# Power table of the S5 layer laid out power-innermost, and the SSD half of the output projection stored gated, with its input added

## Chip, cores and metric

One core of a Trainium2 chip runs the whole model in one launch. The metric is device time in microseconds; the kernel before was run three times (3845.32 to 3852.04, median 3851.29), and one further execution was profiled.

## What is computed

A two-layer model over 2048 latent tokens and 256 context tokens, 1024 features, float32. Layer one projects the normalised input, runs a bidirectional SSD (state-space) group and a windowed attention group with sinks beside it, and projects both together. Layer two is a bidirectional S5 layer (64 groups of 64 complex states, 16 channels) with GLU and gate. Cut to what the change touches:

```
def window_attention(q, k, v, kc, vc, sink):   # blocks of 128 queries
    kb, vb = band(k), band(v)                   # key block before, own, after
    ...                                         # plus all 256 context keys

def even_layer(x, xc, c, c_ctx, ...):
    shift, scale, gate = adaln(c, ada_w, ada_b)          # silu(c) @ ada_w + ada_b
    shift_c, scale_c, gate_c = adaln(c_ctx, ada_w, ada_b)
    ...
    x  = x  + gate   * (jnp.concatenate([ssd_out, att], -1) @ w_out)
    xc = xc + gate_c * (jnp.concatenate([ssd_c, att_c], -1) @ w_out)

def odd_layer(...):
    disc = s5_discretise(lam_re, lam_im, log_step, b_re, b_im)  # powers of ab below
    s_re, s_im, _ = s5_bidir(ug, disc, final_c)
    y = s5_output(s_re, s_im, ug, c_re, c_im, d_skip, glu_w, glu_b) * silu(g)
    x = x + gate * (y @ w_out)
```

## The kernel before

Tokens are handled in 18 tiles of 128 (`NT`; tiles 0 and 1 are context). Every float32 product is made of three TensorE products of a rounded and a residual part (`mm3`, lines 289 to 291); the parts are made by ScalarE (`Copy` to the rounded type) and by VectorE or GpSimd (`lo`, line 274).

The program is a chain of stages. In each, a main generator writes the stage's instructions and `merge` lets side generators put in theirs between, by a budget of modelled TensorE time (`self.pe`, the numbers after `yield`). TensorE's order is that of the writing; the other engines and the DMA queue (all loads and stores go through SyncE, SP below) are put in an order by a simulation of the program when it is built. Each engine works through its own list in order.

- **Attention**, about 1545 to 2350 us. For each query tile and head a score (`score`, lines 1154 to 1160: keys in rounded and residual form `K1`, `KL`, whose three band tiles sit in a ring of `RING` slots beside two context slots; a band that runs over the ring's end is read in two pieces), a softmax (1167, 1168), transposes (1174 to 1178) and the product with the values (1184). `kprep` writes the key tile two ahead. The side generator is `half_proj`: the SSD half of the output projection, 36 outputs of 128 x 512 (`f`, two halves of the columns by 18 tiles), copied from PSUM (line 1347) and stored to `part_d` in DRAM (1348). Between its outputs it computes 16 pieces of modulation (`ada_load`, `ada_mm`: 1024 KB of weights `aw` through one buffer, 32 small products, stored to `mod_d`): four pieces of layer one's gate, then twelve of layer two.
- **Output projection** (`out_proj`), about 2350 to 2690 us. Per tile it loads the input `xr` (1413) and the SSD half `pt` (1415), makes the attention half in PSUM (`ps`, eight times `mm3` for two halves), and for each half adds `pt` to it (VectorE, 1448), multiplies by the gate row (VectorE, 1449) and adds to `xr` (GpSimd, 1450; VectorE in the last tile). The sum is stored to `x1_d`, and ScalarE takes its square sum (1452).
- **S5 operators** (`s5_gen`), a side generator of the output projection and of the first part of layer two's input projection (`odd_proj`), about 2420 to 2905 us. VectorE makes powers 0 to 16 of the 64 x 64 complex eigenvalues by doubling (`pn`), copies them into `pw` (1553, 1555; the direction `d` = 1 backwards), and then for 16 pairs of groups and two directions makes the outer products `O` = C x power (1606 to 1611, 544 elements a partition) and `Gm` = B x power (1625 to 1627, 512 elements). In `pw` the 32 group pairs are innermost, so the power index has a step of 32 floats:

```
pw = cp.tile([P, 2, 2, 17, 32], F32, name="pw")
...
pv = lambda k: pw[:, k, d, ps0:ps0 + 16, p0:p0 + NB].rearrange("p t q -> p q t")[:, :, None, :].to_broadcast(sh)
...
V.tensor_tensor(g[:, k], bv(0), pv(x0), ALU.mult)
V.tensor_tensor(t, bv(1), pv(x1), ALU.mult)
```

`Gm` is transposed by TensorE (`gp`, 1639); `O` and B give the lag kernels (`gl`, 1658).

## Time and profile before

| | us |
|---|---|
| runs, lowest / median / highest | 3845.32 / 3851.29 / 3852.04 |
| the profiled execution, its own time | 3853.33 |
| its span in the profile | 3851.6 |
| TensorE busy over the span | 3454.3 (90%) |
| VectorE busy | 2555.0 (66%) |
| ScalarE busy | 1617.3 (42%) |
| GpSimd busy | 1167.9 (30%) |

The shares are means over stages that have different limits, so the stages are read apart, by windows of time. A busy TensorE is not TensorE at its peak: its products overlap, and their ends are modelled. Idle time of an engine that does not set the end costs nothing.

### The profile page before, as it was taken

Reading aid. Unit: us, or ns where it says so; the run is one execution under the profiler, and the core shown is the slowest. Engines: PE = TensorE matmul, PEld = TensorE weight load, DVE = VectorE, ACT = ScalarE, POOL = GpSimd, SP = SyncE. Lnnn points to the kernel's source line nnn. Section 1 sums busy time; section 2 is a strip of 40 time slices with the busy share of each in tenths; the row PEclk is TensorE's granted clock in tenths of the full one; section 3 lists DMA queues with packets and bytes.
Section 4 is the critical chain, followed back from the end, with each engine's and each line's share of the span. In section 5 each row is a group of like instructions: output and inputs, shape, how many; then the busy total and the mean of one; then the engine's idle time right before and its main releaser. Section 6 shows DMA issues by size and latency. Waiting matters only on the chain.

```text
span 3851.6 us, 68715 instructions
## 1 busy us (share of the span) xinstructions
PE 3454.3 (90%) x25669; PEld 3095.7 (80%) x25669; DVE 2555.0 (66%) x5430; ACT 1617.3 (42%) x3519; POOL 1167.9 (30%) x752
## 2 busy tenths in 40 slices
PE   6989899988999997989999999778799988989999
PEld 4978898978998886767877887556689978979977
DVE  5888876565435445756776777999895499503455
ACT  4544554543312223766667774222222522343321
POOL 3122234332213332375555532422101011132221
PEclk8989999999999998989999999889799999999999
DMA  7755577865666777564543336556878954895453
GB/s 282 229 201 187 191 231 261 258 227 193 225 229 217 264 244 210 151 176 129 147 114 102 98 91 183 166 167 197 240 243 264 301 189 143 270 291 165 127 164 110
DMA packets 664857, 758.28 MB, mean 197 GB/s; under 512 B 76795, under 2 KB 529339, under 8 KB 664523
## 3 DMA queue, kind: packets, MB, share of 16 engines
q1 hardware_dynamic: 664523, 753.88, 62.7%
q8 instruction: 203, 3.33, 0.4%
q14 instruction: 131, 1.07, 0.1%
HBM read 516.58 MB, written 237.15 MB: 196 GB/s over the span
## 4 chain that ended last, share of the span: by engine, by line
PE 34%; DVE 16%; DMA 8%; ACT 3%; issue 3%; SPq 3%; POOL 2%; DVEq 0%; POOLq 0%; ACTq 0%
PE mm L289 3%; PE mm L290 3%; PE mm L291 3%; PE pv L1184 3%; PE pt L1174 3%; PE S L1154 2%; PE gpo L289 1%; PE gpo L291 1%; PE gpo L290 1%; PE S L1156 1%; SPq L2023 1%; DVE sc L1884 1%; DVE Bu L1889 1%; DVE sc L1885 1%; DVE Gm L1625 1%
## 5 line engine op out<-in xcount | busy, mean ns | idle before, releaser
L289 PE MATMUL mm<-xTh,wh 128*128 128x256 f32 (+1 forms) x3320 | 1011.5, 305 | 73.5 <-ACT cR L603 24.7
L290 PE MATMUL mm<-xTl,wh 128*128 128x256 f32 (+1 forms) x3320 | 953.7, 287 | 1.3 <-POOL xTl L274 0.7
L291 PE MATMUL mm<-xTh,wl 128*128 128x256 f32 (+1 forms) x3320 | 953.1, 287 | 1.2 <-DVE wl L274 1.2
L289 PEld LDWEIGHTS mm<-xTh,wh 128*128 128x128 f32 (+1 forms) x3320 | 645.7, 194 | 105.2 <-ACT cR L603 27.0
L290 PEld LDWEIGHTS mm<-xTl,wh 128*128 128x128 f32 (+1 forms) x3320 | 645.5, 194 | 18.0 <-issue 14.7
L291 PEld LDWEIGHTS mm<-xTh,wl 128*128 128x128 f32 (+1 forms) x3320 | 643.8, 194 | 2.6 <-DVE wl L274 1.7
L1178 DVE TENSOR_TENSOR tl<-pt,th 128x512 fp32r<-128x512 f32 x328 | 223.7, 686 | 123.3 <-ACT th L1177 121.5
L1167 DVE TENSOR_SCALAR_CACHE_REDUCE p<-S,nsink 128x640 f32<-128x640 f32 (+2 forms) x288 | 235.1, 819 | 91.2 <-PE S L1156 89.1
L1168 ACT ACTIVATE p<-p,nm 128x640 f32<-128x640 f32 (+2 forms) x288 | 224.4, 779 | 91.5 <-DVE p L1167 89.8
L1174 PE MATMUL pt<-ident,p 128*128 128x128 f32 x1312 | 206.2, 280 | 38.9 <-DVE tl L1178 25.5
L1177 ACT ACTIVATE th<-pt 128x512 fp32r<-128x512 f32 x328 | 193.7, 593 | 110.9 <-PE pt L1174 107.5
L289 PE MATMUL mm<-wh,xTh 128*128 128x256 f32 x720 | 218.6, 304 | 16.4 <-DMA wh<-wk 8.6
L1174 PEld LDWEIGHTS pt<-ident,p 128*128 128x128 f32 x1312 | 158.0, 143 | 79.6 <-issue 35.1
L290 PE MATMUL mm<-wl,xTh 128*128 128x256 f32 x720 | 207.0, 287 | 1.6 <-POOL wl L274 1.0
L291 PE MATMUL mm<-wh,xTl 128*128 128x256 f32 x720 | 206.7, 287 | 0.0
L614 DVE SCALAR_TENSOR_TENSOR cA<-cR,vecs,cA 128x256 f32<-128x256 f32 (+3 forms) x192 | 184.6, 973 | 24.3 <-ACT cA L611 20.8
L946 DVE SCALAR_TENSOR_TENSOR rf<-rb,s_P,rf 128x128 f32<-128x128 f32 x288 | 123.8, 475 | 98.6 <-ACT rf L942 96.3
L401 POOL TENSOR_TENSOR xin<-xin,shr 128x1024 f32<-128x1024 f32 x33 | 88.1, 2680 | 316.1 <-DVE xin L400 311.2
L289 PEld LDWEIGHTS mm<-wh,xTh 128*128 128x128 f32 x720 | 141.5, 197 | 23.7 <-DVE zt L577 9.5
L274 POOL TENSOR_TENSOR wl<-w,wh 128x1024 fp32r<-128x1024 f32 (+1 forms) x43 | 99.9, 2326 | 193.9 <-ACT wh L282 163.4
L576 ACT ACTIVATE tz<-mm 128x256 f32<-128x256 f32 x144 | 54.2, 378 | 227.5 <-PE mm L291 227.4
L1184 PE MATMUL pv<-th,vv 128*128 128x512 f32 x328 | 147.8, 451 | 1.7 <-ACT sA L1116 1.0
(459 smaller groups left out, 9057.2 us busy)
## 6 DMA issues: line engine op xcount, KB each, us to landing
wh<-wk SPq DMA_DIRECT2D x116, 512.0 KB
wl<-wk SPq DMA_DIRECT2D x116, 512.0 KB
wk<-wh SPq DMA_DIRECT2D x56, 512.0 KB
wk<-wl SPq DMA_DIRECT2D x56, 512.0 KB
w<-in_e_w_in_dram SPq DMA_DIRECT2D x40, 512.0 KB
xin<-in_x_dram SPq DMA_DIRECT2D x38, 512.0 KB
rf<-prow_d SPq DMA_DIRECT2D x72, 256.0 KB
rb<-prow_d SPq DMA_DIRECT2D x72, 256.0 KB
```

The source lines that it names most:

```text
L274: eng.tensor_tensor(out, x, hi.bitcast(F32), ALU.subtract)
L289: mm(ps, lhsT=ah, rhs=bh, start=first, stop=False)
L290: mm(ps, lhsT=ah, rhs=bl, start=False, stop=False)
L291: mm(ps, lhsT=al, rhs=bh, start=False, stop=last)
L614: nc.vector.scalar_tensor_tensor(acc[:, q:q + m], R[:, s + j:s + j + m], cw[:, 12 * j + b:12 * j + b + 1], acc[:, q:q + m], op0=ALU.mult, ...
L946: V.scalar_tensor_tensor(rf[:, h], rb[:, h], self.s_P[:, c, 16 + hh:17 + hh], rf[:, h], op0=ALU.add, op1=ALU.min)
L1167: V.tensor_scalar(p[:, :w], s, -0.125, nsink[:, h:h + 1], op0=ALU.mult, op1=ALU.min, accum_out=nm)
L1168: A.activation(p[:, :w], p[:, :w], AF.Exp, bias=nm, scale=-1.0, accum_out=d["sm"][:, h:h + 1])
L1174: T.transpose(pt[:, n, :], Ps[h4][:, j * P:(j + 1) * P], self.ident)
L1177: A.activation(th, pt, AF.Copy)
L1178: V.tensor_tensor(tl, pt, th.bitcast(F32), ALU.subtract)
L1184: T.matmul(pv, lhsT=VV[kt][:, hk, :], rhs=t.rearrange("p a b -> p (a b)"), start=first and x == 0, stop=last and x == 1)
```

## The change

- `s5_gen`: `pw` becomes [.., 32, 17], the power innermost; four copies with permuted or reversed addresses take the place of the one at 1553 and the seventeen at 1555; the readers `pv` follow.
- `half_proj`: the output is multiplied by the gate row on its way out of PSUM and the input `xr3` is added by GpSimd before the store. So the four gate pieces come first, each behind a wait of modelled time; a gate row `g3` and an input tile `xr3` (one buffer each) are loaded.
- `out_proj`: `xr` is no longer loaded; VectorE multiplies PSUM by the gate and adds `pt`, two instructions as before; GpSimd's addition is gone.
- `RING` is 5.

```diff
@@ -1037,7 +1037,7 @@
 
         nc, i, tc = self.nc, self.i, self.tc
         V, G, A, T = nc.vector, nc.gpsimd, nc.scalar, nc.tensor
-        RING = 6
+        RING = 5
         with ExitStack() as st:
             e = st.enter_context
 
@@ -1330,12 +1330,24 @@
                     X = xprep(0)
                     z = None
                     if half == 0:
-                        yield ("until", self.pe + HL)
+
+                        for _ in range(4):
+                            z = ada_load()
+                            yield ("until", self.pe + HL)
+                            ada_mm(z)
+                            yield 1.5
+                        z = None
+                    gate = hp.tile([P, 512], F32, name="g3", bufs=1)
+                    self.modrow(gate, "e", 1, 2, half * 512, 512)
                     for t in range(NT):
                         if z:
                             ada_mm(z)
                             yield 1.5
                         z = ada_load() if t + 1 < NT else None
+                        xr = hp.tile([P, 512], F32, name="xr3", bufs=1)
+                        nc.sync.dma_start(xr, (i["ctx"][t * P:(t + 1) * P] if t < 2 else i["x"][(t - 2) * P:(t - 1) * P])[:, half * 512:half * 512 + 512])
+                        if t == 2:
+                            self.modrow(gate, "e", 0, 2, half * 512, 512)
                         xh, xl = X
                         if t + 1 < NT:
                             X = xprep(t + 1)
@@ -1344,7 +1356,8 @@
                             self.mm3(ps, xh[:, k, :], xl[:, k, :], W[k][0], W[k][1], k == 0, k == 7)
                             yield 0.65
                         y = hp.tile([P, 512], F32, name="y3", bufs=2)
-                        V.tensor_copy(y, ps)
+                        V.tensor_tensor(y, ps, gate, ALU.mult)
+                        G.tensor_tensor(y, y, xr, ALU.add)
                         nc.sync.dma_start(self.part_d[t * P:(t + 1) * P, half * 512:half * 512 + 512], y)
                         yield 0.2
             ORDER = [q for q in range(2, NT) if q < CTX] + [0, 1] + [q for q in range(2, NT) if q >= CTX]
@@ -1410,7 +1423,6 @@
         for t in range(NT):
             xh, xl = X
             xr = row("xr")
-            nc.sync.dma_start(xr, i["ctx"][t * P:(t + 1) * P, :] if t < 2 else i["x"][(t - 2) * P:(t - 1) * P, :])
             pt = row("pt")
             nc.sync.dma_start(pt, self.part_d[t * P:(t + 1) * P, :])
             if t + 1 < NT:
@@ -1445,9 +1457,8 @@
                     yield 0.43
             for h in range(2):
                 hs = slice(h * 512, h * 512 + 512)
-                V.tensor_tensor(pt[:, hs], ps[h], pt[:, hs], ALU.add)
-                V.tensor_tensor(pt[:, hs], pt[:, hs], gate[:, hs], ALU.mult)
-                (V if t == NT - 1 else G).tensor_tensor(xr[:, hs], xr[:, hs], pt[:, hs], ALU.add)
+                V.tensor_tensor(xr[:, hs], ps[h], gate[:, hs], ALU.mult)
+                V.tensor_tensor(xr[:, hs], xr[:, hs], pt[:, hs], ALU.add)
             nc.sync.dma_start(self.x1_d[t * P:(t + 1) * P, :], xr)
             A.activation(pt, xr, AF.Square, accum_out=ss[:, t:t + 1])
             if t == 1:
@@ -1549,10 +1560,11 @@
             V.tensor_tensor(o(1), o(1), t1[:, :m], ALU.add)
             m *= 2
 
-        pw = cp.tile([P, 2, 2, 17, 32], F32, name="pw")
-        V.tensor_copy(pw[:, :, 0], pn[:, :, :, 0:32])
-        for t in range(17):
-            V.tensor_copy(pw[:, :, 1, 16 - t, :], pn[:, :, t, 32:64])
+        pw = cp.tile([P, 2, 2, 32, 17], F32, name="pw")
+        for k in range(2):
+            V.tensor_copy(pw[:, k, 0].rearrange("p q t -> p t q"), pn[:, k, :, 0:32])
+            w = pw[:, k, 1]
+            V.tensor_copy(bass.AP(tensor=w.tensor, offset=w.offset + 16, ap=[list(w.ap[0]), [-1, 17], [17, 32]]), pn[:, k, :, 32:64])
         V.tensor_copy(self.AR, pn[:, 0, 16, :].rearrange("p (a b) -> p a b", a=2))
         V.tensor_scalar(self.AI[:, 0], pn[:, 1, 16, :].rearrange("p (a b) -> p a b", a=2), -1.0, None, op0=ALU.mult)
         V.tensor_copy(self.AI[:, 1], pn[:, 1, 16, :].rearrange("p (a b) -> p a b", a=2))
@@ -1600,7 +1612,7 @@
                 Os.append(O.rearrange("p k q t c -> p k q (t c)"))
                 sh = [P, NB, 17, 16]
                 t = wk.tile(sh, F32, tag="Ot", name="Ot", bufs=1)
-                pv = lambda k: pw[:, k, d, :, p0:p0 + NB].rearrange("p t q -> p q t")[:, :, :, None].to_broadcast(sh)
+                pv = lambda k: pw[:, k, d, p0:p0 + NB, :, None].to_broadcast(sh)
                 cv = lambda k: C[:, k, p0:p0 + NB, None, :].to_broadcast(sh)
                 for (k, x0, x1, s) in ((0, 0, 1, None), (1, 1, 0, -1.0)):
                     V.tensor_tensor(O[:, k], cv(0), pv(x0), ALU.mult)
@@ -1619,7 +1631,7 @@
                 sh = [P, NB, 16, 16]
                 t = wk.tile([P, NB, 17, 16], F32, tag="Ot", name="Ot", bufs=1)[:, :, 0:16, :]
                 ps0 = 0 if d == 0 else 1
-                pv = lambda k: pw[:, k, d, ps0:ps0 + 16, p0:p0 + NB].rearrange("p t q -> p q t")[:, :, None, :].to_broadcast(sh)
+                pv = lambda k: pw[:, k, d, p0:p0 + NB, None, ps0:ps0 + 16].to_broadcast(sh)
                 bv = lambda k: Bb[:, k, d, p0:p0 + NB, :, None].to_broadcast(sh)
                 for (k, x0, x1, op) in ((0, 0, 1, ALU.subtract), (1, 1, 0, ALU.add)):
                     V.tensor_tensor(g[:, k], bv(0), pv(x0), ALU.mult)
```

TensorE at the place where `half_proj` begins, before (`f` is an output of the SSD half, `wh`, `wl` the weights, `x3h`, `x3l` the transposed SSD output, `S` a score, `pt` the transposed softmax, `pv` the product with the values):

```order
9314 L1160 LDWEIGHTS identb
9315 L1160 MATMUL S<-maskb,identb 128x128
9316 L1154 MATMUL S<-K_17000,sA 128x256
9317 L1156 MATMUL S<-KL,sA 128x256
9318 L1174 MATMUL pt<-ident,p 128x128 x4
9319 L289 MATMUL f<-wh_17146,x3h 128x512
9320 L290 MATMUL f<-wl_17147,x3h 128x512
9321 L291 MATMUL f<-wh_17146,x3l 128x512
```

And with the change (`af` is a piece of the modulation, `aw` its weights, `cvs` the conditioning vector):

```order
9314 L1160 LDWEIGHTS identb
9315 L1160 MATMUL S<-maskb,identb 128x128
9316 L1154 MATMUL S<-K_17000,sA 128x256
9317 L1156 MATMUL S<-KL,sA 128x256
9318 L1174 MATMUL pt<-ident,p 128x128 x4
9319 L365 MATMUL af<-aw,cvs 32x64 x32
9320 L1184 MATMUL pv<-th,vv 128x512
9321 L1184 MATMUL pv<-tl,vv 128x512
```

Where the first output of the SSD half began now stands the first of four gate pieces; 46 to 57 other rows lie between one and the next, and the first `f` comes after the fourth. From the first product of the output projection on, TensorE's order is the same as before.

GpSimd at the end of the attention and the start of the output projection, before (`gt`, `o`: the attention's own gate and output; `x3p`: the transposed attention output, residual part):

```order
438 L1225 TENSOR_TENSOR o<-o,gt 128x1024
439 L274 TENSOR_TENSOR x3p<-x_27072,x3p 128x1024
440 L274 TENSOR_TENSOR x3p<-x_27150,x3p 128x1024
441 L1450 TENSOR_TENSOR xr<-xr,pt 128x512 x2
442 L274 TENSOR_TENSOR x3p<-x_27290,x3p 128x1024
443 L1450 TENSOR_TENSOR xr<-xr,pt 128x512 x2
444 L274 TENSOR_TENSOR x3p<-x_27358,x3p 128x1024
445 L1450 TENSOR_TENSOR xr<-xr,pt 128x512 x2
```

And with the change (`y`: the tile on its way to `part_d`):

```order
471 L1224 TENSOR_TENSOR gt<-gt,rb__26809 128x1024
472 L1225 TENSOR_TENSOR o<-o,gt 128x1024
473 L1360 TENSOR_TENSOR y_26932<-y_26932,xr_26708 128x512
474 L1360 TENSOR_TENSOR y_27130<-y_27130,xr_26947 128x512
475 L274 TENSOR_TENSOR x3p<-x_27249,x3p 128x1024
476 L274 TENSOR_TENSOR x3p<-x_27324,x3p 128x1024
477 L274 TENSOR_TENSOR x3p<-x_27461,x3p 128x1024
478 L274 TENSOR_TENSOR x3p<-x_27526,x3p 128x1024
```

The pairs `xr` between two `x3p` are gone, and the additions to `y` stand in the attention's list instead, 36 of them, between the rotations of queries and keys and the gates.

The DMA queue SP in the attention, with the change (line numbers of the changed kernel; before, 1348 was the store to `part_d`):

```order
1025 L1296 DMA an<-in_o_norm_w_dram 128x1x64
1026 L1361 DMA part_d<-y_19009 128x512
1027 L1348 DMA xr_19137<-in_x_dram 128x512
1028 L1324 DMA x_19450<-ysT_d 128x8x128
1029 L1292 DMA ab<-in_o_ada_b_dram 128x1x64
1030 L1075 DMA sin<-in_k_sin_dram 128x128
```

A store to `part_d` now waits for GpSimd's addition where it waited for VectorE's copy, and the load of the next `xr` stands right behind it.

## Rows read from the trace of the kernel before

**Rows 1.** busy us by stage: window, length, PE, PEld, DVE, ACT, POOL, clock, DMA, GB/s

```profile
1545.00:2350.00 805.00, 751.22 (x5522) 617.74 (x5521) 570.52 (x1178) 558.27 (x1124) 402.59 (x237) 0.98 0.45 121
2350.00:2425.00 75.00, 65.56 (x276) 51.15 (x275) 52.76 (x107) 26.47 (x34) 23.21 (x13) 0.91 0.90 268
2425.00:2690.00 265.00, 196.81 (x1169) 151.25 (x1168) 255.10 (x316) 51.68 (x104) 88.24 (x39) 0.87 0.54 168
2690.00:2925.00 235.00, 197.92 (x1899) 183.38 (x1898) 213.02 (x282) 63.34 (x153) 10.53 (x4) 0.89 0.82 248
```

**Rows 2.** the chain that ended last, shares by line, 2350 to 2930 us

```profile
by line: DVE Gm L1625 8.1%; issue 7.8%; DVE Ot L1626 6.8%; DVE O L1606 4.8%; DVE Gm L1627 4.5%; DVE Ot L1607 4.5%; PE mm L289 3.4%; DVE pt L1449 3.2%; PE mm L290 3.2%; PE mm L291 3.1%; DVE pt L1448 2.9%; DVE O L1609 2.8%; DMA xin<-x_d 2.3%;
```

**Rows 3.** TensorE by line, 2425 to 2690 us (count, busy us, mean ns, idle before)

```profile
L1639 PE MATMUL gp<-ident,Gm 128*128 128x128 f32 x108 | 22.0, 321 | 60.2 <-DVE Gm L1627 60.2
```

**Rows 4.** VectorE by line and form, 2425 to 2690 us

```profile
L1625 DVE TENSOR_TENSOR Gm<-Bb,pw 128x512 f32<-128x512 f32 x33 | 41.9, 1314 | 3.6 <-PE gp L1639 3.6
L1626 DVE TENSOR_TENSOR Ot<-Bb,pw 128x512 f32<-128x512 f32 x30 | 33.9, 1132 | 0.6
L1606 DVE TENSOR_TENSOR O<-C,pw 128x544 f32<-128x544 f32 x32 | 31.0, 1009 | 0.0
L1449 DVE TENSOR_TENSOR pt<-pt,gate 128x512 f32<-128x512 f32 x28 | 26.4, 956 | 0.0
L1607 DVE TENSOR_TENSOR Ot<-C,pw 128x544 f32<-128x544 f32 x31 | 25.2, 814 | 0.6
L1627 DVE TENSOR_TENSOR Gm<-Gm,Ot 128x512 f32<-128x512 f32 x30 | 23.8, 794 | 0.7
L1448 DVE TENSOR_TENSOR pt<-ps,pt 128x512 f32<-128x512 f32 x27 | 18.1, 682 | 2.2 <-PE ps L291 2.2
```

**Rows 5.** the same, 2690 to 2925 us

```profile
L1626 DVE TENSOR_TENSOR Ot<-Bb,pw 128x512 f32<-128x512 f32 x34 | 36.7, 1079 | 0.7
...
L1607 DVE TENSOR_TENSOR Ot<-C,pw 128x544 f32<-128x544 f32 x33 | 23.8, 723 | 0.7
L1627 DVE TENSOR_TENSOR Gm<-Gm,Ot 128x512 f32<-128x512 f32 x34 | 23.4, 688 | 0.6
L1606 DVE TENSOR_TENSOR O<-C,pw 128x544 f32<-128x544 f32 x32 | 21.6, 717 | 0.3 <-PE gl L1658 0.3
```

**Rows 6.** GpSimd additions among VectorE's work (start us, us)

```profile
2488.31 3.29 POOL L1450 TENSOR_TENSOR xr<-xr,pt 128x512 f32<-128x512 f32 x2 [1.32 <-DVE pt L1449]
2488.70 1.78 DVE L1609 TENSOR_TENSOR O<-O,Ot 128x544 f32<-128x544 f32 x1
...
2490.52 1.67 DVE L1607 TENSOR_TENSOR Ot<-C,pw 128x544 f32<-128x544 f32 x1
```

**Rows 7.** GpSimd by line and form, 2425 to 2690 us

```profile
L1450 POOL TENSOR_TENSOR xr<-xr,pt 128x512 f32<-128x512 f32 x26 | 46.5, 1799 | 48.0 <-DVE pt L1449 35.5 <-DMA lag_d<-lg 12.5
L274 POOL TENSOR_TENSOR x3p<-x,x3p 128x1024 fp32r<-128x1024 f32 x12 | 41.0, 3414 | 121.0 <-ACT x3p L1392 81.4 <-DVE pt L1448 13.6 <-issue 13.2
```

**Rows 8.** single lines over the run (ns: least, median, greatest; first and last start)

```profile
L1449 DVE TENSOR_TENSOR pt<-pt,gate x36: 674/680/2915, 2382.0 to 2684.1; 128x512 f32<-128x512 f32 x36
...
L1450 POOL TENSOR_TENSOR xr<-xr,pt x34: 1282/1680/2891, 2382.7 to 2672.1; 128x512 f32<-128x512 f32 x34
...
L1555 DVE COPY pw<-pn x17: 181/184/2385, 2358.4 to 2460.6; 128x64 f32<-128x64 f32 x17
```

**Rows 9.** VectorE by line and form, 1545 to 2350 us

```profile
L1347 DVE COPY y<-f 128x512 f32<-128x512 f32 x36 | 24.7, 687 | 5.8 <-PE f L291 5.4
```

**Rows 10.** TensorE: a score in three pieces, then one in two (start us, us)

```profile
2199.92 0.22 PE L1154 MATMUL S<-K,sA 128*128 128x128 f32 x1
...
2200.81 0.60 PE L1174 MATMUL pt<-ident,p 128*128 128x128 f32 x4
...
2250.64 0.34 PE L1154 MATMUL S<-K,sA 128*128 128x384 f32 x1
...
2251.40 0.39 PE L289 MATMUL f<-wh,x3h 128*128 128x512 f32 x1
```

## The prediction

> **What bounds the kernel now.** I read busy time by stage first [rows 1], since the shares of the whole span mix stages with different limits. In the attention (1545 to 2350 us) TensorE is busy 751 of 805 us, VectorE 571, GpSimd 403: TensorE sets the pace and the other two have room. From 2425 to 2690 us, call it stage A, it is the other way round: VectorE is busy 255 of 265 us, TensorE 197, at a granted clock of 0.87, and GpSimd 88. From 2690 to 2925 us, stage B, VectorE has 213 of 235 us, TensorE 198, and the DMA engines a share of 0.82, so three resources lie close together. Next the chain of waits from 2350 to 2930 us [rows 2]: its three heaviest lines that belong to the S5 generator are the `Gm` products 1625 and 1626 (14.9% together) and the `O` product 1606; 1449 of the output projection has 3.2%. TensorE's waits say the same from its side: in A it stood 60.2 us before the transposes of `Gm`, and VectorE's 1627 released it [rows 3]. So in A a microsecond of VectorE is about a microsecond of the program, in B less, and in the attention nothing.
>
> **The power layout.** In `Gm` the innermost operand index is the power, and its step was 32 floats. Where GpSimd is nearly idle 1626 takes 1079 ns for 512 elements; 1627, the same number of elements with no such step, takes 688 ns [rows 5]. The product 1606 works on the same table, but there the power is not the innermost index, and 544 elements take 717 ns [rows 5]. So I charge the difference of 0.39 us to the step, and expect 1625 and 1626 at 0.69 us after. They run 63 times in A [rows 4]: 63 x 0.39 = 24.6 us. The loops make 64 of each, 128 in all, so some 65 are left for B: 25.4 us. The `O` products change only in a middle step: nothing. The building of `pw` had seventeen copies of a median 184 ns [rows 8], 3.1 us, and one larger; the four new copies have permuted addresses, which no row shows. Four of 544 elements cost at most 4 x 1.08 = 4.3 us by 1626, at least nothing: I take no change, and 4 us lie inside the range.
>
> **The gated half.** In the output projection VectorE had two instructions an output half (1448 and 1449) and has two after, both of 512 elements: no change, except that in the last tile the two additions of line 1450 that ran on VectorE go, 2 x 0.7 = 1.4 us by the length of 1448 [rows 4]. What goes besides is GpSimd's addition. GpSimd is not the bound, but its additions lengthen VectorE's instructions: next to one pair of 1450, which took 3.29 us, a 1609 took 1.78 us and a 1607 1.67 us [rows 6], where 1607 alone takes 0.72 [rows 5]. That is about 1.0 us for each addition, and with 26 in A [rows 7] 26 us. The other way: the mean of each form in A [rows 4] over its mean in B [rows 5], or over its median [rows 8] for 1449, and 1079 for 1625, times its count, gives 7.8 (1625) + 1.6 (1626) + 9.3 (1606) + 7.7 (1449) + 2.8 (1607) + 3.2 (1627) = 32.4 us, and of GpSimd's time in A 1450 had 46.5 of 87.5 us [rows 7], the residual parts `x3p` the rest, which stay: 0.53 x 32.4 = 17 us. I take 20 us, nearer to the count over all instructions than to the one pair.
>
> A page makes this term larger. The Trainium skill ("SBUF — State Buffer", section "SBUF: two separate sides") says that GpSimd and a VectorE instruction with two SBUF inputs take a shared port pair as an exclusive lock for a whole instruction. By it each addition could hold VectorE up for its full length; what that would give is the third rival, from rows alone. At the one pair shown the trace comes near it, 1.0 us for an addition that takes at least 1.28 [rows 8]; over all instructions it does not.
>
> Stage A therefore loses 24.6 + 20 + 1.4 = **46 us** of VectorE work. VectorE then needs 209 of the 219 us that are left (its 10 us of idle time kept), and TensorE's 197 us, which the low clock of 0.87 has stretched, still fit: VectorE stays the bound, so I count all of it. In stage B TensorE has at most 37 us of room and the DMA engines 0.18 x 235 = 42 us, and both are needed by the projection whose order does not change; of the 25.4 us I count half, **13 us**, with 0 and 25 as ends. In the burst at the start of the output projection, with a DMA share of 0.90 [rows 1], the loads of the first `xr` go, 512 KB each at 268 GB/s or 2 us; some additions go too. TensorE is busy 66 of 75 us there, so I take **1 us**, between 0 and 5.
>
> **What the attention pays.** Multiplying on the way out of PSUM costs VectorE what the copy did (687 ns [rows 9] against 682 for 1448, also PSUM with one SBUF operand [rows 4]). The 36 additions are at least 1.28 us each [rows 8], 46 us more for a GpSimd busy 403 of 805: hidden, if none holds others up. The input comes in 36 loads of 256 KB instead of 18 of 512, the same bytes, at a DMA share of 0.45 [rows 1]; SP issues 18 more and four gate rows. With a ring of five, five of the inner query tiles have a band over the end instead of four, and the last tile's band is cut too: 2 tiles x 16 heads. A score in three pieces takes 0.89 us from its first product to what follows, one in two 0.76 [rows 10]: 32 x 0.13 = 4 us of the engine that sets the pace. The four gate pieces come first, behind one weight buffer: 1024 KB at 121 to 268 GB/s [rows 1] is 4 to 9 us, and the next load can start only when the last piece is done. Some 50 other rows of TensorE lie between two pieces, which should cover most; three waits of 0 to 9 us are 0 to 27, and I take 4, near the lower end because that other work is there. In all **8 us** lost.
>
> **Sum.** 3853.3 (the profiled execution) - 46 - 13 - 1 + 8 = 3801; the median of the runs shown is 2 us under that execution, so 3799, and I say 3800. Its own range reaches from 3765 (26 instead of 20, all of B, 5 at the start, nothing paid: 3851 - 52 - 25 - 5 = 3769, less the 4 us of copies) to 3826 (17 instead of 20, nothing in B, 15 paid, 4 for the copies: 3851 - 43 - 1 + 15 + 4).
>
> **Rivals.**
> - *TensorE and the DMA engines take over early.* TensorE's order keeps `Gm` transposes among the projection's products, and each must still wait for the last of its VectorE chain; speaking for it: 197 busy of 265 us in A, and B's three near-limits. Against: the 60 us before 1639. Two thirds of A, nothing of B: 3851 - 30 - 1 + 8 = 3828.
> - *The layout saves nothing*, because the other operand of `Gm`, B with a broadcast inner index, makes it slow. For it: no row shows that broadcast alone in `Gm`. Against: 1606 has such a broadcast, at 717 ns. Left are 20 + 1.4 + 1 less 8: 3837.
> - *Each addition of 1450 had held VectorE for its whole length.* 26 x 1.28 = 33 us [rows 7, 8] instead of 20: 3787. For it, besides the page: greatest durations of 2.9 us in 1449 beside a median of 0.68 [rows 8]. Against: the 32.4 us counted above for all GpSimd work together.
> - *Slower: the chain behind an output.* PSUM, multiply, GpSimd add, store: the store to `part_d` stands in SP before loads of queries and keys, and waits for a GpSimd whose list holds rotations of 128 x 1024 elements. If an output is late by x, what the next query tile loads is late too, and TensorE, the bound there, stands. 36 outputs x 2 us = 72: 3872. It decides from 51 / 36 = 1.4 us an output. Against it: queries are loaded a tile ahead, and GpSimd is idle half of the time.
>
> **Chances.** The forecast 0.53; TensorE and DMA early 0.20; the lock 0.13; the layout 0.07; slower 0.07. The range 3765 to 3832 (the first rival with 4 us for the copies) takes in the forecast and the two at 0.20 and 0.13, 0.86 together, and leaves the other two out. A measurement of this kernel tells about 0.2%, some 8 us, from no change. Faster by more holds in all cases but the slower one, 0.93, less their edges: 0.92. That one is split: a mild form ends within 0.2%, 0.03 with the edges, and slower keeps 0.05.
>
> **What would show it.** Right: 1625 and 1626 at a median near 0.69 us, GpSimd in A below 50 us, means of 1606 and of the multiply near their medians, A shorter by 40 to 50 us at a higher clock, the wait before the `Gm` transposes well under 60 us, the attention longer by under 15. Wrong: 1625 still at 1.08; A shorter by less than 30 with TensorE busy throughout; waits of TensorE in the attention behind `af` or behind scores whose keys or queries came late; SP waiting for GpSimd before stores to `part_d`.

## Result and profile after

The changed kernel takes 3786.77 us (median of 4 runs, 3782.45 to 3792.56) against 3851.66 for the kernel before beside it: ratio 0.9831, 95% interval 0.9817 to 0.9845, 65 us faster. The profiled execution took 3789.91 us, its span 3788.1 (before 3851.6); TensorE is busy 3447.3 us of it (91%), VectorE 2477.5 (65%), ScalarE 1614.5 (43%), GpSimd 1146.1 (30%).

To see where 63.5 us of span went I cut both traces at marks that do not depend on time: the first score and the last product with the values bound the attention, the first and last product of the output projection bound the next stage, and the piece of layer two's input projection that still runs beside the S5 generator lasts until layer two's first `ips` product (called the odd stage below; it contains stage B). Windows of the kernel before (window, length, busy time of PE, PEld, DVE, ACT, POOL, then granted clock, DMA share, GB/s; in the rows PE is TensorE and PEld its weight loads, DVE is VectorE, ACT ScalarE, POOL GpSimd):

```profile
1525.70:2349.70 824.00, 760.35 (x5570) 625.88 (x5568) 585.70 (x1200) 572.13 (x1152) 417.66 (x252) 0.97 0.46 125
2356.10:2674.10 318.00, 251.34 (x1375) 192.63 (x1376) 288.02 (x398) 70.19 (x124) 110.33 (x51) 0.88 0.60 184
2674.10:2977.60 303.50, 256.29 (x2406) 239.16 (x2405) 248.69 (x321) 81.93 (x192) 23.25 (x10) 0.90 0.82 250
```

The same three of the changed kernel:

```profile
1534.30:2337.10 802.80, 755.59 (x5634) 629.68 (x5633) 583.18 (x1200) 568.30 (x1152) 462.57 (x288) 0.98 0.52 141
2344.70:2619.90 275.20, 245.34 (x1376) 190.34 (x1377) 237.82 (x385) 73.26 (x127) 45.94 (x18) 0.93 0.60 181
2619.90:2920.60 300.70, 258.86 (x2406) 239.81 (x2405) 216.45 (x314) 80.06 (x189) 21.01 (x8) 0.90 0.82 250
```

Attention 21.2 us shorter, output projection 42.8, odd stage 2.8. What is left (8.6 us more ahead of the attention, 6.5 less behind the odd stage, 1.2 more between two stages) lies in unchanged code. It looks like scatter between executions: no edit of this document lies ahead of the attention, and yet in the twelve profiles its first score starts anywhere from 1520.6 to 1536.5 us. Two things deserve a look. In the output projection VectorE lost 50 us of work and the stage 43 us. In the attention TensorE's busy time hardly moved (760 to 756, although it has 64 more products), so most of the 21 us is idle time that went: 63.7 us of it before, 47.2 after. I had forecast a loss there.

VectorE by line and form in the changed kernel, 2400 to 2635 us, which answers to [rows 4] (1637 to 1639 are the former 1625 to 1627, 1618 and 1619 the former 1606 and 1607, 1460 and 1461 the former 1448 and 1449):

```profile
L1637 DVE TENSOR_TENSOR Gm<-Bb,pw 128x512 f32<-128x512 f32 x36 | 29.6, 866 | 1.8 <-PE gp L1651 1.8
...
L1461 DVE TENSOR_TENSOR xr<-xr,pt 128x512 f32<-128x512 f32 x30 | 23.7, 808 | 0.0
L1618 DVE TENSOR_TENSOR O<-C,pw 128x544 f32<-128x544 f32 x32 | 23.4, 765 | 0.3 <-PE gl L1670 0.3
L1638 DVE TENSOR_TENSOR Ot<-Bb,pw 128x512 f32<-128x512 f32 x31 | 23.4, 753 | 0.6
...
L1460 DVE TENSOR_TENSOR xr<-ps,gate 128x512 f32<-128x512 f32 x30 | 20.2, 684 | 9.3 <-PE ps L291 9.2
```

The means are still above 0.69 us because of a few long instructions; least, median and greatest over the whole run show it. From the views of single lines, first the kernel before:

```profile
L1625 DVE TENSOR_TENSOR Gm<-Bb,pw x64: 1017/1084/3298, 2468.7 to 2896.2; 128x512 f32<-128x512 f32 x64
L1626 DVE TENSOR_TENSOR Ot<-Bb,pw x64: 1006/1086/2209, 2493.0 to 2917.3; 128x512 f32<-128x512 f32 x64
L1553 DVE COPY pw<-pn x1: 714/714/714, 2456.9 to 2456.9; 128x1088 f32<-128x1088 f32 x1
```

and the changed kernel:

```profile
L1637 DVE TENSOR_TENSOR Gm<-Bb,pw x64: 677/684/2910, 2452.5 to 2828.1; 128x512 f32<-128x512 f32 x64
L1638 DVE TENSOR_TENSOR Ot<-Bb,pw x64: 675/691/2718, 2471.4 to 2849.8; 128x512 f32<-128x512 f32 x64
L1460 DVE TENSOR_TENSOR xr<-ps,gate x36: 673/682/693, 2367.1 to 2623.6; 128x512 f32<-128x512 f32 x36
L1461 DVE TENSOR_TENSOR xr<-xr,pt x36: 673/680/2893, 2368.6 to 2625.4; 128x512 f32<-128x512 f32 x36
L1565 DVE COPY pw<-pn x2: 666/668/671, 2437.2 to 2444.2; 128x544 f32<-128x544 f32 x2
L1567 DVE COPY pw<-pn x2: 691/692/692, 2437.7 to 2444.7; 128x544 f32<-128x544 f32 x2
```

TensorE's wait before the transposes of `Gm`, 60.2 us before [rows 3], is 24.0 in the window 2400 to 2635 us:

```profile
L1651 PE MATMUL gp<-ident,Gm 128*128 128x128 f32 x112 | 20.9, 302 | 25.8 <-DVE Gm L1639 24.0 <-ACT Gev L1655 1.6
```

In that window GpSimd has, apart from one small memset, only the residual parts of [rows 7] left, at 2.7 us each instead of 3.4:

```profile
L274 POOL TENSOR_TENSOR x3p<-x,x3p 128x1024 fp32r<-128x1024 f32 x13 | 35.4, 2726 | 165.0 <-ACT x3p L1405 165.0
```

GpSimd's 36 additions now stand in the attention and cost there what was expected of them (window 1534 to 2337 us):

```profile
L1360 POOL TENSOR_TENSOR y<-y,xr 128x512 f32<-128x512 f32 x36 | 46.5, 1291 | 61.0 <-DVE y L1359 33.4 <-PE pt L1174 15.4 <-PE S L1156 11.6
```

### The profile page after: what moved, and what is told of

Same layout as the page of the kernel before. It is cut to its first block, busy times and chain, and to the rows that moved or that the text cites. A ratio compares the mean times of both kernels' runs of the same rounds, so it can differ in the third digit from the quotient of the medians.

```text
span 3788.1 us, 68824 instructions
## 1 busy us (share of the span) xinstructions
PE 3447.3 (91%) x25733; PEld 3100.0 (82%) x25733; DVE 2477.5 (65%) x5414; ACT 1614.5 (43%) x3519; POOL 1146.1 (30%) x754
## 3 DMA queue, kind: packets, MB, share of 16 engines
q1 hardware_dynamic: 667691, 754.93, 63.5%
q14 instruction: 131, 1.07, 0.1%
## 4 chain that ended last, share of the span: by engine, by line
PE 30%; DVE 13%; DMA 7%; SPq 2%; issue 2%; ACT 2%; POOL 1%; DVEq 0%; ACTq 0%; POOLq 0%
PE pv L1184 3%; PE pt L1174 3%; PE S L1154 2%; PE mm L289 2%; PE gpo L291 2%; PE gpo L290 2%; PE gpo L289 2%; PE S L1156 2%; PE mm L290 2%; PE mm L291 2%; DVE sc L1896 1%; PE f L289 1%; PE f L291 1%; PE f L290 1%; DVE sc L1899 1%
## 5 line engine op out<-in xcount | busy, mean ns | idle before, releaser
L946 DVE SCALAR_TENSOR_TENSOR rf<-rb,s_P,rf 128x128 f32<-128x128 f32 x288 | 135.0, 514 | 97.8 <-ACT rf L942 92.1
L408 PE MATMUL tp<-ident,xin 128*128 128x128 f32 x432 | 93.9, 304 | 63.7 <-DVE xTl L274 44.8
```

The lines of the kernel that those rows point to most:

```text
L946: V.scalar_tensor_tensor(rf[:, h], rb[:, h], self.s_P[:, c, 16 + hh:17 + hh], rf[:, h], op0=ALU.add, op1=ALU.min)
```

## Experiments

### The change in its parts

Four kernels from the kernel before: the power layout alone; the gated half with the gate pieces that it needs and the ring of five, in the old layout; the ring alone; the gate pieces alone, drawn ahead of the half product. Each edit is the piece of the diff above that its name says; the last two are short:

```diff
 r_only, of the kernel before
-        RING = 6
+        RING = 5
...
 q_only, of the kernel before
                     if half == 0:
-                        yield ("until", self.pe + HL)
+                        for _ in range(4):
+                            z = ada_load()
+                            yield ("until", self.pe + HL)
+                            ada_mm(z)
+                            yield 1.5
+                        z = None
```

> The kernel before with the power layout alone; everything else as before. If the parts simply add, this run has 63 x 0.39 = 25 us of the output projection's gain and about 3 us of the stretch behind it: 28 us less than before, the attention the same to 5 us, the median of the Gm products 0.69 us, GpSimd's additions still lengthening the multiply of the output projection (mean above 0.9 us). Rival: GpSimd's additions hide what the layout saves (a shorter list on VectorE runs into them more often): less than 15 us. Second rival: VectorE was the only bound and the additions cost nothing: 45 us or more.

> The kernel with the change, but with the power layout as before: the gated half with its input and the ring of five. If the parts add: 65 - 28 = 37 us less than before, of which some 20 in the attention and 18 to 22 in the output projection. If the attention's 21 us in the one trace are chance, 15 to 20 us in all.

> The kernel before with a ring of five key tiles, nothing else. By the count of extra score pieces 32 x 0.13 = 4 us slower. Rival: the other order that the build gives to the engines' lists makes the attention shorter, which would be up to 20 us faster; in that case the gain of the attention is the list's and not the gated half's.

> The kernel before with the four gate pieces written ahead of the SSD half, nothing else (the half is still copied and stored ungated, the ring is six). Theory: the attention's gain comes from this order, because the modulation pieces no longer stand between the outputs in the first half and the outputs spread more evenly: 10 to 20 us faster than before, all of it before the output projection. Rival: the pieces wait for their weights, as the prediction had it: 0 to 8 us slower. Second rival: no difference, and the gain comes from the gating or the ring.

Measured beside 19 runs of the kernel before (median 3849.79 us; the last row beside 4, as above); stage lengths from one profiled execution of each, which need not be a typical one: that of the layout alone is the slowest of its six runs (3836.18 us, median 3826.15), that of the gated half the fastest of its six (3816.35, median 3823.97).

| kernel | ratio, 95% interval | attention | output projection | odd stage |
|---|---|---|---|---|
| before | 1 | 824.0 | 318.0 | 303.5 |
| power layout alone | 0.9938 (0.9915 to 0.9962) | 821.7 | 302.2 | 293.3 |
| gated half, ring of five | 0.9931 (0.9911 to 0.9950) | 802.3 | 297.4 | 311.4 |
| ring of five alone | 0.9953 (0.9935 to 0.9970) | 804.8 | 318.7 | 305.6 |
| gate pieces first alone | 1.0013 (0.9999 to 1.0027) | 816.0 | 318.7 | 306.1 |
| all | 0.9831 (0.9817 to 0.9845) | 802.8 | 275.2 | 300.7 |

The layout and the gated half each shorten the output projection, by 15.8 and 20.6 us, and the two together by 42.8. The layout alone gave less there than the 25 us expected: with GpSimd's additions still in place the multiply 1449 rose from 32.4 to 37.7 us of VectorE, so part of what the `Gm` products saved seems to have gone to instructions that now met the additions; without the additions the layout is worth 22.2 us (297.4 to 275.2). By the medians the two parts give 24 and 26 us (28 and 37 were expected), 49 together, and the whole change 65. 6.4 us of that difference lie in the output projection, as just read; where the rest lies is not shown. The gate pieces give nothing that can be told from no change, so the expected 10 to 20 us did not come. The surprise is the ring: a number that I had costed only by its extra score pieces makes the kernel 19 us faster by itself, and the attention 19 us shorter; in the two other kernels that have it the attention is 21 to 22 us shorter.

### Why a shorter ring helps

A ring of five gives TensorE more to do, so the gain must be a wait. ScalarE works its list in the order of the build. In the attention that list mixes softmax (1168), the rounding of the transposed softmax (`th`, 1177) and the key copies (1100), which need the rotation that GpSimd makes (1080). ScalarE's waits in the attention (1500 to 2370 us; total us, times, longest), the kernel before:

```profile
ACT K L1100 <- POOL kraw L1080: 33.4, 10, 4.7
```

the ring of five alone:

```profile
ACT K L1100 <- POOL kraw L1080: 3.7, 1, 3.7
```

Layout alone and gate pieces alone, which keep the ring, have 34.0 and 36.3 us in 10 waits; the gated half with the ring of five and the whole change have 3.7 in one. One of the ten waits in the kernel before (start us, us; idle time before in brackets):

```profile
1722.58 0.73 POOL L1080 TENSOR_TENSOR kraw<-kraw,kraws 128x256 f32<-128x256 f32 x1
...
1723.35 0.86 ACT L1100 ACTIVATE K<-kraw 64x256 fp32r<-64x256 f32 x2 [4.10 <-POOL kraw L1080]
...
1724.23 1.06 ACT L1327 ACTIVATE x3h<-x 128x1024 fp32r<-128x1024 f32 x1
1725.19 0.81 ACT L1168 ACTIVATE p<-p,nm 128x640 f32<-128x640 f32 x1
...
1726.00 0.58 ACT L1177 ACTIVATE th<-pt 128x512 fp32r<-128x512 f32 x1
...
1726.61 0.69 DVE L1178 TENSOR_TENSOR tl<-pt,th 128x512 fp32r<-128x512 f32 x1 [4.05 <-ACT th L1177]
...
1727.45 0.63 PE L1174 MATMUL pt<-ident,p 128*128 128x128 f32 x4 [3.39 <-DVE tl L1178]
```

The copy stands at the head of ScalarE's list 4.1 us before GpSimd ends the rotation. Behind it wait a softmax and a `th` whose inputs are there; VectorE's `tl` then waits for `th`, and TensorE's next transposes for `tl`, 3.4 us. Nobody needs that copy soon: query tile 4 is at work, and the keys are those of token tile 9, first read by query tile 8. (The program writes `kprep` two tiles ahead, so this copy stands at query tile 7 there; the build's simulation has moved it forward.) The trace names VectorE as the releaser of TensorE, VectorE names ScalarE, and only ScalarE's row names the cause.

With six slots the copy of tile 9 takes the place of tile 3, last read by query tile 4; with five that of tile 4, last read by query tile 5. The build's simulation, in which a copy must wait for that reading, therefore puts the copy further back in ScalarE's list: in the ring-alone trace the first copy that moves starts 186.6 us after the first score instead of 162.4, its rotation over at 160.7 as before (160.3). By then there is nothing to wait for.

If that is the mechanism, the same gain must come without a shorter ring. Four more kernels:

```diff
 k_late, of the kernel before (ring of six)
+            ONE = {}
...
-                        A.activation(kh, src, AF.Copy)
+                        if kt - 4 in ONE:
+                            A.activation(kh, src, AF.Copy, scale=ONE[kt - 4][par * 64:par * 64 + 64])
+                        else:
+                            A.activation(kh, src, AF.Copy)
...
                 d = st_.pop(qt)
+                ONE[qt] = qp.tile([P, 1], F32, name="one", bufs=4)
+                V.tensor_scalar(ONE[qt], d["nm"][:, NH - 1:NH], 0.0, 1.0, op0=ALU.mult, op1=ALU.add)
...
 split6, of the kernel before (ring of six)
-                    while j + n < nb and slot(kts[j + n]) == slot(kts[j]) + n:
+                    while j + n < nb and (kts[j + n] - 2) % 5 and slot(kts[j + n]) == slot(kts[j]) + n:
...
 six_plain, of the changed kernel
-        RING = 5
+        RING = 6
...
-                        w = hp.tile([P, 512], F32, name="w3", bufs=2)
+                        w = hp.tile([P, 512], F32, name="w3", bufs=1)
...
-                        y = hp.tile([P, 512], F32, name="y3", bufs=2)
+                        y = hp.tile([P, 512], F32, name="y3", bufs=1)
```

(`six_late` is `six_plain` with the edit of `k_late`. The scale is one; it makes the copy of tile kt wait for the last score of query tile kt - 4, as a ring of five does.)

> The kernel before, ring of six, with one dependence added: from key tile 6 on, ScalarE's four key copies take as their scale a column of ones that VectorE makes from the last score minimum of query tile kt-4, so the build cannot list them before that tile's scores. No score is split further, no work is taken away (14 tiny VectorE operations are added). Theory A (the gain of the ring of five is the place of the copies in ScalarE's list): the wait of the copy for GpSimd's rotation falls from 33.4 us in 10 waits to under 6, TensorE's idle time in the attention from 63 to about 50, and the attention from 824 to about 798 (the ring alone gave 805 and paid some 5 us in split scores): ratio about 0.994, 23 us faster. Rival B (the shorter ring itself, its buffers or its split scores, made the gain): the wait may go, but the attention stays at 818 to 826, ratio 0.999 to 1.001. Rival C (the copies come too late for the scores and GpSimd's low parts): the attention is longer than 826, ratio over 1.001.

> The kernel before, ring of six, with the scores of six more query tiles cut in one more piece, at the places at which the ring of five cuts them; the copies and their waits stay. Theory A: a cut costs 0.15 us a score on TensorE (two pieces 0.76, three 0.89 us before, 2.4 us per tile of 16 heads in the ring of five), so the attention becomes 14 us longer, 838, where TensorE sets the pace, and at least 5 longer if some of it falls into waits; the wait of the copies for the rotation stays at 30 to 36 us; ratio 1.0013 to 1.004. Rival B (the cuts themselves made the ring's gain, by spreading the softmax): attention under 820, ratio under 0.999.

> The changed kernel with a ring of six again and the key copies put late by the dependence on the scores of tile kt-4; room for the sixth slot comes from one buffer instead of two for the half product's result and for its weights' stage. Theory A (the place of the copies is all that the ring of five gave): the attention is shorter than with five, by the 5 us of the split scores and up to 9 more that the dependence gave over the ring in the kernel before (791 against 805), so 789 to 797 where the changed kernel has 801 to 803; output projection 275, as there; ratio 0.979 to 0.982, 5 to 14 us under the changed kernel. Rival: the single buffers make the half product's stores and weight copies wait and give back 5 to 10 us: ratio 0.982 to 0.984.

> The same with the ring of six and the single buffers, but without the dependence, so that the copies stand where the build puts them by itself. Theory A: the copies stand at the end of the rotation again, ScalarE waits for GpSimd's rotation 30 us or more in about ten waits, and the attention is 815 to 825; ratio 0.986 to 0.990, 12 to 25 us over the changed kernel. Rival (the ring of five had to do with its two buffers' room alone, or the place does not matter once the gate is in): attention 797 to 806, ratio 0.982 to 0.984.

| kernel | ratio, 95% interval | attention | wait of the copies for the rotation |
|---|---|---|---|
| ring of six, copies late | 0.9940 (0.9928 to 0.9952) | 791.3 | 3.9 us, once |
| ring of six, six more tiles cut | 1.0018 (1.0006 to 1.0030) | 832.5 | 37.3 us, 10 times |
| changed kernel, ring of six | 0.9899 (0.9878 to 0.9920) | 833.1 | 32.3 us, 9 times |
| the same, copies late | 0.9833 (0.9810 to 0.9856) | 795.8 | 3.3 us, once |

ScalarE's wait and the attention's window with the copies late, in the kernel before:

```profile
ACT K L1104 <- POOL kraw L1081: 3.9, 1, 3.9
```

```profile
1532.00:2323.30 791.30, 747.97 (x5570) 618.12 (x5568) 581.24 (x1218) 577.24 (x1152) 417.81 (x252) 0.98 0.48 130
```

and in the changed kernel with a ring of six, copies where the build puts them:

```profile
ACT K L1100 <- POOL kraw L1080: 32.3, 9, 4.9
```

```profile
1531.10:2364.20 833.10, 761.46 (x5571) 628.08 (x5569) 592.01 (x1200) 570.40 (x1152) 461.74 (x288) 0.97 0.50 136
```

The late copies alone, with nothing taken away and 18 tiny VectorE instructions added, make the kernel before 0.6% faster, 26 us by the medians (3828.10 against 3853.67); TensorE's idle time in the attention falls from 63.7 to 43.3 us, and its busy time from 760 to 748. The cuts alone make it slower. In the changed kernel, giving back the sixth slot lengthens the attention by 30 us, and the dependence takes 37 away again, with the same single buffers in both. So the place of the copies is shown to be the cause, in both kernels. The cut cost less than I wrote: 8.0 us more TensorE time for 96 scores (768.39 against 760.35, at a granted clock of 0.98 against 0.97), some 0.08 us each instead of 0.15:

```profile
1520.60:2353.10 832.50, 768.39 (x5762) 644.43 (x5760) 586.01 (x1200) 572.19 (x1152) 417.07 (x252) 0.98 0.46 124
```

The version with six slots and late copies has the shorter attention but is no faster than the changed kernel (3785.44 us, 0.9833, against 3786.77, 0.9831), so I found nothing that beats it. I had expected 5 to 14 us; the rival written beside it, that the single buffers give the gain back, fits the total but was not tried by itself. The changed kernel with six slots came out slower in the attention than the 815 to 825 us expected (833), its ratio within what was expected.

### What the moved additions cost VectorE

```diff
 pool_add, of the changed kernel
+        junk = ww.tile([P, 170], F32, name="junk")
...
                 V.tensor_tensor(xr[:, hs], xr[:, hs], pt[:, hs], ALU.add)
+                if t < NT - 1:
+                    for c in range(3):
+                        G.tensor_tensor(junk, gate[:, c * 170:c * 170 + 170], gate[:, 512 + c * 170:682 + c * 170], ALU.add)
```

> The changed kernel with work added that nobody waits for: after each of the 34 halves of 17 tiles of the output projection GpSimd adds two pieces of the resident gate row into a scratch tile, three instructions of 170 columns each, about what the moved addition read and wrote in the kernel before. Theory A (the moved addition cost VectorE time by running beside it): VectorE's two-input operations that overlap with it become longer again, VectorE's busy time in the output projection rises by 17 to 26 us over the changed kernel's and the stage by 10 to 20, from 275 to 285 to 295; ratio to the kernel before 0.986 to 0.988. Rival B (the gain of that part came from the shorter chain behind the last product and the loads that no longer wait, not from contention): busy time and stage stay within 4 us of the changed kernel, ratio 0.982 to 0.984. Rival C (one engine locks the other out for all its time): busy time up by 33 or more, stage 300 or more, ratio 0.990 or more.

> The changed kernel as it is, to stand beside the three others in the same call. Both theories: ratio 0.983, within 0.0015; attention 803, output projection 275, the stage behind it 301 us, each within 4 us, if the stage times of single profiles are to be read as closely as they were.

With the additions back on GpSimd, without anyone waiting for them, the kernel goes from 0.9832 (0.9817 to 0.9847; the changed kernel again) to 0.9866 (0.9852 to 0.9881). Output projection of the changed kernel run again, then with the added work:

```profile
2341.80:2617.70 275.90, 242.96 (x1376) 187.67 (x1377) 236.86 (x385) 72.97 (x127) 43.87 (x18) 0.94 0.61 180
```

```profile
2342.90:2634.10 291.20, 249.06 (x1376) 190.06 (x1377) 257.59 (x386) 73.10 (x127) 118.35 (x120) 0.91 0.57 171
```

VectorE does one instruction more and is busy 20.7 us longer, and the stage is 15.3 us longer. That GpSimd's additions slow VectorE by running beside it is thereby shown. How they do it stands in the trace of the kernel before (VectorE's and GpSimd's rows of two additions):

```profile
2610.86 0.68 DVE L1448 TENSOR_TENSOR pt<-ps,pt 128x512 f32<-128x512 f32 x1
2611.08 1.28 POOL L1450 TENSOR_TENSOR xr<-xr,pt 128x512 f32<-128x512 f32 x1 [2.56 <-DVE pt L1449]
2611.47 1.47 DVE L1606 TENSOR_TENSOR O<-C,pw 128x544 f32<-128x544 f32 x1
...
2615.18 0.68 DVE L1627 TENSOR_TENSOR Gm<-Gm,Ot 128x512 f32<-128x512 f32 x1
2615.33 1.66 POOL L1450 TENSOR_TENSOR xr<-xr,pt 128x512 f32<-128x512 f32 x1 [2.98 <-DVE pt L1449]
2615.89 1.68 DVE L1607 TENSOR_TENSOR Ot<-C,pw 128x544 f32<-128x544 f32 x1
```

Each engine waits for the other's instruction to end. 1606 starts while the first addition runs and ends 0.58 us behind it, little less than the 0.72 us that it takes alone. The second addition starts while 1627 runs, which has both inputs in SBUF, and takes 1.66 us instead of 1.28; the first, which started beside 1448 with one input in PSUM, was not held up. In the window of [rows 4], 25 of the 26 additions end within a lengthened VectorE instruction, 26.8 us above the least lengths of such instructions, 1.07 us each.

So the 20.7 us against GpSimd's 73.9 us for the added work are no price per microsecond. The 73.9 us contain GpSimd's own waits (an addition of 170 columns takes 542 ns at least and 725 in the mean), and VectorE waits only for an instruction that began before its own. The added pieces are a third as long as the additions that they stand for, and some ran beside the generator's small set-up operations instead of the outer products, so that 20.7 lies near my 20 is luck. Two pairs of kernels differ in the additions themselves (and in the ring and the gate pieces, which belong to the attention). The output projection with the layout alone, and with the gated half alone:

```profile
2364.10:2666.30 302.20, 250.70 (x1376) 192.46 (x1377) 270.59 (x387) 71.62 (x126) 101.09 (x52) 0.90 0.63 195
```

```profile
2339.20:2636.60 297.40, 252.83 (x1375) 195.03 (x1376) 258.97 (x399) 71.95 (x126) 45.63 (x18) 0.89 0.56 164
```

Without the 34 additions VectorE is busy 29.1 us less in the old layout (288.0 to 259.0) and 32.8 less in the new one (270.6 to 237.8).

## Why the prediction came out as it did

The forecast was 3800, the result 3787; it lies within the range. That is in part luck: a miss of 29 us one way stands against some 17 us the other. By terms:

- **Stage A, 46 us of VectorE.** Right in sum, by two errors that offset each other. VectorE lost 50.2 us in the output projection and the stage 42.8, at a granted clock of 0.93 instead of 0.88. The step went as written, from medians of 1.084 and 1.086 us to 0.684 and 0.691. But the layout took 17.4 us off VectorE in this stage with the additions in place and 21.2 without them, not 24.6. And the 20 us for contention were too few: 26.8 in the prediction's own window by the instructions, 29.1 and 32.8 over the stage by the two pairs of kernels. The reading of the one pair, 1.0 us an addition or 26, was the better one; the 17 us against it counted six lines of VectorE only. The lock rival, 33 us and a total of 3787, met the total by chance, for the attention came 29 us better than it had it and the odd stage 10 worse. Its mechanism is in the trace; its price, the whole 1.28 us of every addition, is somewhat too high, 1.07 here, since VectorE's instruction starts after the addition and so waits for less than all of it.
- **Stage B, 13 us: too large.** The odd stage lost 2.8 us. VectorE fell by 32 us there, but the two other limits of [rows 1] stayed: TensorE 259 of 301 us, DMA 0.82. One profile does not give this term well, so I take all twelve: with the old layout the odd stage was 302.8 to 311.4 us (six kernels, mean 305.4), with the new one 289.8 to 302.6 (six, mean 297.3). The layout is worth some 8 us, of which the changed kernel kept 3. The mis-sized step is "of the 25.4 us I count half". It took TensorE's room as fixed, but TensorE's time for the same products went with the granted clock: 263 us at 0.88, 256 to 259 at 0.89 and 0.90, 252 to 253 at 0.92. Among the six with the new layout, the three at 0.90 lie at 300.7 to 302.6 us, the three at 0.92 at 289.8 to 295.4. In the old layout 0.92 gave hardly anything: the kernel before with late copies has it and took 302.8 us. The layout alone, then the late copies:

```profile
2666.30:2959.60 293.30, 253.32 (x2406) 236.25 (x2405) 220.20 (x318) 80.46 (x190) 21.45 (x8) 0.92 0.83 256
```

```profile
2649.60:2952.40 302.80, 252.92 (x2407) 236.14 (x2406) 247.46 (x321) 81.61 (x192) 23.31 (x10) 0.92 0.82 251
```

That the clock is why the changed kernel kept only 3 us is argued from these profiles, not tried; what sets the clock at 0.90 or 0.92 stays open.
- **Start, 1 us, and the copies, 0.** Too small to be told apart by stage. The four copies took 2 x 0.668 + 2 x 0.692 = 2.7 us; the eighteen before had taken 7.4 in the trace, the seventeen small ones a mean of 447 ns and not their median of 184. So the copies gained 4.7 us, which are part of VectorE's 50.
- **Attention, 8 us lost: wrong by 29 us.** The failed step is "2 tiles x 16 heads", with its 32 x 0.13 = 4 us, taken as all that the ring does. The sum costed what TensorE executes and overlooked that the number of slots decides when the build may place a copy. The size of the cut was nearly right (32 x 0.08 = 2.6 us). The wait of 33 us was in the trace before, among ScalarE's waits, and the prediction gives ScalarE no word: busy 572 of 824 us, it has room. It had, but not at those ten places. The other 4 us, for the gate pieces, did not show: that kernel's attention was 8 us shorter than the one before, its median 6 us longer, and the interval of its ratio holds 1.
- **Slower by the store chain.** Not seen: GpSimd's additions waited 33 us for the multiply; SP waited 81 us for them before its stores to `part_d`, where it had waited 99 for VectorE's copy; TensorE idled less than before, not more.
- **The two other rivals.** That TensorE and the DMA engines take over early is near what stage B shows, 2.8 us of 13 in the one profile, and not what A shows, whose stage lost 42.8. That the layout saves nothing is contradicted by the medians of 1637 and 1638 and by the kernel with the layout alone.

Against the sum of 52 us the span lost 63.5: 29 more by the attention, less 10 in the odd stage, 4 in the output projection and its start, and 3 in unchanged stretches.

## What to carry to other kernels

Where an engine works a fixed list, an idle gap is charged to whoever is waiting last; follow the releasers back until an instruction appears whose result nobody needs yet. Such an instruction is better placed late, and a dependence on something that is finished late does it almost without work. And a buffer count is an edit of the order: before costing a ring or pool size by its traffic alone, compare where the build puts the instructions that wait for a slot.

## What the runs showed of the hardware

Two things that I had not expected:

- VectorE's instructions with one operand in PSUM were not touched by GpSimd at all: 1460 took 673 to 693 ns in 36 executions (6 of them beside a GpSimd instruction), and 1448 before it 672 to 692 (12 of 36), while 1461, right behind 1460 with both operands in SBUF, reached 2893. The Trainium skill ("SBUF — State Buffer", section "SBUF: two separate sides") names two SBUF inputs as one condition for a lock against GpSimd, held for a whole instruction by whichever starts first; here the trace agrees on both. In the output projection of the kernel before, 30 VectorE instructions of 512 and 544 elements with both inputs in SBUF started beside a GpSimd instruction and took over 0.1 us more than their least. Of these, 23 without the long step ended 0.55 to 0.59 us after that instruction, where their own least is 0.67 to 0.71 us, and the 7 of 1625 and 1626 ended 0.88 to 1.00 us after it, with a least of 1.01 to 1.02. The 16 others that started so were not lengthened; there GpSimd's instruction was the longer one, 2.2 to 2.9 us instead of 1.28 or 3.0 to 8.7 instead of 2.35.
- What a step costs depends on where it stands. Reading the power table at a step of 32 floats cost 0.39 us in 512 elements of a product. The new copies, one writing at a step of 17 floats and one in reversed order at that step, took 0.67 and 0.69 us for 544 elements, no more than a product without steps (0.717, [rows 5]). But the copy 1553 before, which wrote without a step, took 0.714 us for 1088, so per element the new ones take nearly twice as long; whether the step or the shape of the copy costs that was not tried.
